# Last group norm moved ahead by two gate tiles, the mixed projection's pools split, its input tiles on another queue, x loads spread

## The chip, the cores and the metric

The kernel runs on one core of a Trainium2 chip. Times are device microseconds of that core. TensorE (PE in the profile) does the matrix products, VectorE (DVE) and ScalarE (ACT) the element-wise work, GpSimd (POOL) a few additions and part of the DMA issues, and SyncE (SP) issues DMAs only. A DMA is issued by one of these engines, in that engine's own instruction order: while the instruction at the head of a queue waits, those behind it wait as well.

## What is computed

One layer of a hybrid encoder for 384 tokens (256 of a prompt, 8 streams of 16 sampled tokens), model width 2048, all in float32:

```python
u = rmsnorm(x, g_mix_pre)
proj = u @ w_in                               # pool | z | xBC | dt | gates
a_pool = pool_mixer(pool part)                # windows 2, 4, 8, 16, then a map per group
a_ssd  = gated_rmsnorm(ssd_scan(...) , z)     # 8 groups of 512 channels, each normed by itself
merged = sigmoid(gA) * (a_pool @ w_pool_proj) + sigmoid(gB) * (a_ssd @ w_ssd_proj)
x = x + rmsnorm(merged @ w_out, g_mix_post)
x = x + rmsnorm(relu(rmsnorm(x) @ w_up)**2 @ w_down, g_mlp_post)
```

The scan also returns new states. The outputs are y and the new pool, convolution and scan states.

## The kernel before

**Products.** Each float32 operand is split into a high part h (rounded by ACT to a shorter float) and a rest l (subtracted by DVE); a product is the sum of three matmuls, h·h, h·l and l·h. A weight tile of 128 x 1024 is fetched by SP (`wfetch`, L61 to L64), its h is made by ACT (L70) and its l by DVE (L71). There are three buffers each for the fetched tile, h and l, so a fetch waits for the l of the tile three earlier. A "unit" is such a tile: `half` (L101 to L103) runs 24 matmuls on it, and a gate or projection tile of 128 channels has two units.

**Order of the work.** The framework plans one fixed order of instructions for each engine before the kernel runs, from the program order and its own estimates of time: an instruction that it believes ready can be put ahead of one that comes first in the program. An instruction that uses a tile of a new pool has its place in that order only behind the release of the older pools whose addresses it covers. At run time every instruction waits just for the tiles that it needs itself (pools with `reuse_waits="tile"`). `behind(ins)` adds an order edge and no wait: what is traced in its block stands behind `ins` on the same engine. `later()` does so behind the latest weight split that was noted in `cut`.

**Stages around the change.** (1) Eight scan groups g = 0 to 7, each with ten projection tiles. A group ends with `finish` (L917; a 512-channel norm: two matmuls for the sum over channels, L207 and L208, then ten dependent DVE instructions, L189 to L193 and L210) and `store` (L920: four DVE products, L925, into the z tiles, and four DMAs by POOL into `a_scr`, L928). For the last group this comes in the branch `g == G`: gate tiles 0 to 3 with the rest of the scan woven in, the last scan products, gate tiles 4 to 7, and then `finish(prev)` and `store(prev)`.

(2) The mixed projection, `a_ssd @ w_ssd_proj`. It is done by a seven-product scheme on 2 x 2 blocks: `quad` splits each step into seven "forms" (b11, b21, U, b22, W, V, X), and for each of eight pairs of channel tiles, gk = 0 to 7, and both column halves there is one quad: 112 forms of 6 or 12 matmuls (L1169 to L1171, N = 512). The forms are woven between the units of the gate tiles 8 to 12 and of twelve tiles of the other gate (`gate_b`, `gate_late`; `hook` runs 3 or 4 forms after each unit, the first three after the second tile's last unit). `load` in `quad` fetches four weight tiles by SP (L1130) and adds one more onto the first by an accumulating DMA of POOL (L1133), which makes U. `aload(gk)` reads one input tile `ax` from `a_scr` by four DMAs (L1229, on SP), `diffs` (L1235, DVE) forms its differences, and `refill` splits them (L1242 ACT, L1243 DVE). The places of these in `extra` are counted by t = 0 to 13 over the fourteen forms of one gk; W, V and X of a gk are refilled at t = 0 to 2 of that gk itself.

All tiles of stage 2 lie in one pool, `phe`, with the accumulators `acs` first (36,864 bytes in each partition), then `ax`, the split inputs, the gate tiles `gt` among them, and the weight tiles `wd` last. The pool lies over `phd`, the pool of the scan groups.

(3) The output projection, `moving` (L154 to L156), four column blocks nb with eight weight tiles `w_wo` each. Ahead of it POOL loads the three x tiles of 1 MB (L1428 and L1429). `gpo`, a scale vector, is fetched by SP at the start of each block (L1522) and scaled by ACT (L1523). The x tiles are first read by `residual` at the end of the fourth block.

Of the kernel before, what the change touches and what calls it, by code (L numbers as in the profile page):

```python
# [14 lines left out]
P = 128  # L15
# [18 lines left out]
def build(ctx, tc, io):  # L34
# [21 lines left out]
    def behind(ins):  # L56
        return nullcontext() if ins is None else tc.issue_after(ins.ins)

    cut = [None, None]

    def wfetch(src, name):  # L61
        w = wpool.tile([P, 1024], F32, tag="w", name=f"w_{name}")
        sy.dma_start(w, src)
        return w, name  # L64

    def wsplit(f):
# [10 lines left out]
    @contextmanager  # L77
    def later():
        with behind(cut[0]), behind(cut[1]):
            yield  # L80
# [502 lines left out]
    def gate_b(i, pool, tag, hook=None, bufs=None):  # L583
        ps = proj([io["w_gb"][i, q] for q in range(2)], xg, f"gb{i}", hook)
        t = pool.tile([P, T], F32, tag=tag, name=f"gbt{i}", **({"bufs": bufs} if bufs else {}))
        with later():
            v.tensor_tensor(halves(t), even_odd(ps), halves(rstd), ALU.mult)
            s.activation(t, t, AF.Sigmoid)
        gp.dma_start(gb_scr[i], t)

    with tc.tile_pool(name="phd", bufs=2, reuse_waits="tile") as pd, tc.tile_pool(
# [325 lines left out]
        def finish(D):  # L917
            D.bc = norm_bc(pd, D.ssum, 512, f"g{D.g}", last[0], D.parts)

        def store(D):  # L920
            bc = D.bc
            for j in range(4):
                i = D.g * 4 + j
                z = D.zs[j]
                v.scalar_tensor_tensor(  # L925
                    out=z, in0=z, scalar=vec[:, V_NRM + i : V_NRM + i + 1], in1=bc, op0=ALU.mult, op1=ALU.mult
                )
                gp.dma_start(a_scr[i], z)  # L928
# [15 lines left out]
        for g in range(G + 1):  # L944
            if g == G:
                S = prev.p[1]
                work = [
                    [lambda: xside(S)],
                    [lambda: hside(S), lambda: eside(S, 0)],
                    [],  # L950
                    [lambda: eside(S, 1)],
                    [lambda: dside(S)],
                    [lambda: expside(S)],
                    [lambda: fside(S, 0), lambda: fside(S, 1)],
                    [],
                ]
# [12 lines left out]
                state(prev.p[1])  # L969
                final(prev.p[1])  # L970
                for i in range(4, 8):
                    gate_b(i, pd, "cacc")
                prev.parts = None
                finish(prev)
                store(prev)
                break
            u0 = 17 + g * 10
            D = Pair()
# [138 lines left out]
    def split(w, name):  # L1117
        h = wpool.tile([P, 1024], F32R, tag="wh", name=f"wh_{name}")
        l = wpool.tile([P, 1024], F32R, tag="wl", name=f"wl_{name}")
        s.activation(h, w, AF.Copy)  # L1120
        v.tensor_tensor(l, w, h.bitcast(F32), ALU.subtract)
        return h, l

    def quad(nm, pool, acc, np_, fresh, unit, part, extra=lambda i: None):
# [92 lines left out]

    mpool = ExitStack()
    phe = ExitStack()
    pq = phe.enter_context(tc.tile_pool(name="phe", bufs=1, reuse_waits="tile"))  # L1220
    acc = pq.tile([P, 18, 512], F32, name="acs")
    KEYS = {"b11": (0,), "s2": (2,), "b21": (3, 5), "U": (6,), "b22": (8, 9), "W": (7,), "V": (1,), "X": (4,)}
    raw, slots = [], [{} for _ in range(8)]

    def aload(gk):
        x = pq.tile([P, 10, 2, P], F32, tag="ax", name=f"ax{gk}")
        for q in range(2):
            for p in range(2):
                sy.dma_start(x[:, q * 3 : q * 3 + 3, p], a_scr[gk * 4 + q * 2 + p].rearrange("p (s t) -> p s t", s=3))  # L1229
        raw.append(x)  # L1230

    def diffs(gk):
        x = raw[gk]
        for o, a, b in DIFFS:
            v.tensor_tensor(x[:, o], x[:, a], x[:, b], ALU.subtract)  # L1235

    def refill(gk, key):
        ss = KEYS[key]
        n = len(ss)
        src = raw[gk][:, ss[0] : ss[-1] + 1 : max(1, ss[-1] - ss[0])]  # L1240
        h, l = (pq.tile([P, n, 2, P], F32R, tag=f"a{a}{key}", name=f"a{a}{key}{gk}", bufs=2 if key == "s2" else 1) for a in "hl")
        s.activation(h, src, AF.Copy)  # L1242
        v.tensor_tensor(l, src, h.bitcast(F32), ALU.subtract)  # L1243
        for i, j in enumerate(ss):
            slots[gk][j] = (h[:, i], l[:, i])

    def sp_quad(gk, np_):
        def part(slot, k2):
            h, l = slots[gk][slot]
            return h[:, k2], l[:, k2]  # L1250

        def extra(i):
            t = np_ * 7 + i
            if gk and t < 3:
# [22 lines left out]
        return quad(f"sq{gk}_{np_}", pq, acc, np_, gk == 0, lambda i, nb: io["w_ssd"][nb, gk * 2 + i], part, extra)  # L1277

    todo, place = [], {}

    def fetch(n):
        if n not in place:
            place[n] = pq.tile([P, 1024], F32, tag="wd", name=f"mw{n}", bufs=7)
        gp.dma_start(place[n][:, :T], gb_scr[n])
        gp.dma_start(place[n][:, T : 2 * T], ma_scr[n])

# [67 lines left out]

    for i in range(8, 10):
        gate_b(i, pq, "gt", hook, 2)
    for i in range(4, KD):
        gate_late(i, hook)
    for i in range(10, 13):
# [65 lines left out]
        return y  # L1425

    blk = lambda i: slice(i * 512, i * 512 + 512)
    for b in range(3):  # L1428
        gp.dma_start(x1[:, b, :], io["x_tok"][b])  # L1429
    xs2 = []  # L1430

    def xtiles(pool, n):
# [6 lines left out]
    with tc.tile_pool(name="phf", bufs=1, side="right", reuse_waits="tile") as pf, tc.tile_pool(  # L1439
# [80 lines left out]
        for nb in range(4):  # L1520
            gpo = pf2.tile([P, 512], F32, tag="gpo", name=f"gpo{nb}", bufs=1)
            sy.dma_start(gpo, io["g_mix_post"][blk(nb)].partition_broadcast(P))  # L1522
            s.activation(gpo, gpo, AF.Copy, scale=-0.5)  # L1523
            o = [sstile(f"wo{nb}_{b}") for b in range(3)] if nb else o_first

            def scaled(b, nb, o, gpo):
                return v.tensor_tensor(hm[:, b, blk(nb)], o[b], gpo, ALU.mult)

            def done(b):
                q = pf2.tile([P, 512], F32, tag="q", name=f"q1_{nb}_{b}", bufs=1)  # L1530
                sq = lambda: s.activation(q, o[b], AF.Square, accum_out=st[:, b, nb : nb + 1])
                if nb < 3:
                    sq()
                    scaled(b, nb, o, gpo)
                    return
                act(sq)
                with behind(ca[0]), behind(cd[0]):
                    ys[b] = postnorm(pf2, st, b, "n1", doubled=True)
                ca[0], cd[0] = root[0], root[1]
                if b == 2:  # L1540
                    return
                for i in range(3):
                    residual(b, i)
                dve(lambda: scaled(b, nb, o, gpo))
                residual(b, 3)
                if b == 1:
                    square(0, 0)
# [386 lines left out]
```

## Time and profile before

| | |
|---|---|
| median of 3 runs | 2600.66 us (2598.7 to 2602.01) |
| the profiled execution | 2600.41 us, its span 2598.4 us |
| PE | 2575.4 us busy, 99% of the span |
| PEld (weight loads) | 2447.4 us, 94% |
| DVE | 1952.1 us, 75% |
| ACT | 1597.8 us, 61% |
| POOL | 424.0 us, 16% |
| DMA | 490.42 MB, 189 GB/s over the span |

PE is busy for nearly the whole span, so the table says little about where time could go. The windows view gives the busy time of each engine in chosen stretches together with the mean clock that was granted to TensorE (1.00 is full). The timeline lists instructions with their start, their length and, in brackets, the idle time of their engine before them and what ended it. Times in these views are in us from the start of the span.

### The profile page before, as it was taken

How to read it: one execution, taken by the hardware profiler on the slowest of the kernel's cores; microseconds unless marked ns; L12 is line 12 of the kernel's file. 1: busy time of each engine (PE TensorE's matmuls, PEld its weight loads, DVE VectorE, ACT ScalarE, POOL GpSimd, SP SyncE). 2: the span in 40 equal slices, each digit the busy share in tenths (PEclk: the TensorE clock that was granted, in tenths of full speed). 3: DMA queues.
4: the chain of work that ended last, by engine and by line, in shares of the span. 5: the costliest groups of instructions: out<-in, count | busy, mean ns of one | idle time of the engine just before them, and what ended most of it. 6: DMA issues, size and time to landing. Idle time of an engine off the chain costs nothing.

```text
span 2598.4 us, 41070 instructions
## 1 busy us (share of the span) xinstructions
PE 2575.4 (99%) x15589; PEld 2447.4 (94%) x15589; DVE 1952.1 (75%) x2763; ACT 1597.8 (61%) x2520; POOL 424.0 (16%) x622
## 2 busy tenths in 40 slices
PE   9999999999999999989999999999999999999998
PEld 9999999999999999978988988999999999999997
DVE  6676367999999999678888855767777777777766
ACT  6443355657565756467887634667667666666653
POOL 0000043445444544100000210000000000000000
PEclk9999999999999999999999999999999999999999
DMA  7444466666676676576766565655455554455434
GB/s 279 151 136 160 161 227 213 232 212 232 228 241 208 230 241 223 180 241 194 212 199 183 175 220 178 196 168 156 146 162 163 167 166 146 154 157 166 140 137 171
DMA packets 151189, 490.42 MB, mean 189 GB/s; under 512 B 21728, under 2 KB 36896, under 8 KB 145232
## 3 DMA queue, kind: packets, MB, share of 16 engines
q1 hardware_dynamic: 111312, 358.29, 40.9%
q0 software_dynamic: 32624, 114.70, 15.3%
q10 hardware_dynamic: 7056, 14.81, 1.8%
q8 instruction: 122, 2.00, 0.3%
q14 instruction: 75, 0.61, 0.1%
HBM read 437.85 MB, written 49.87 MB: 188 GB/s over the span
## 4 chain that ended last, share of the span: by engine, by line
PE 93%; DMA 2%; issue 2%; DVE 2%; ACT 1%; POOL 0%; SPq 0%; DVEq 0%; POOLq 0%; ACTq 0%
PE pj_up L101 6%; PE pj_up L102 6%; PE pj_up L103 6%; PE wd L1171 5%; PE wd L1170 5%; PE wd L1169 5%; PE pj_x L101 5%; PE pj_x L102 5%; PE pj_x L103 5%; PE pj_z L101 3%; PE pj_z L103 3%; PE pj_z L102 3%; PE sq L1170 2%; PE sq L1171 2%; PE sq L1169 2%
## 5 line engine op out<-in xcount | busy, mean ns | idle before, releaser
L101 PE MATMUL pj_up<-x1h,wh_up 128*128 128x384 f32 (+1 forms) x1024 | 333.7, 326 | 0.0
L102 PE MATMUL pj_up<-x1l,wh_up 128*128 128x384 f32 (+1 forms) x1024 | 333.5, 326 | 0.0
L103 PE MATMUL pj_up<-x1h,wl_up 128*128 128x384 f32 (+1 forms) x1024 | 333.5, 326 | 0.0
L70 ACT ACTIVATE wh_up<-w_up 128x1024 fp32r<-128x1024 f32 x126 | 133.1, 1057 | 219.2 <-PE pj_up L102 206.1
L101 PE MATMUL pj_x<-xgh,wh_x 128*128 128x384 f32 x768 | 252.0, 328 | 0.0
L103 PE MATMUL pj_x<-xgh,wl_x 128*128 128x384 f32 x768 | 250.4, 326 | 0.0
L102 PE MATMUL pj_x<-xgl,wh_x 128*128 128x384 f32 x768 | 250.4, 326 | 0.0
L71 DVE TENSOR_TENSOR wl_up<-w_up,wh_up 128x1024 fp32r<-128x1024 f32 x126 | 153.9, 1221 | 56.3 <-ACT wh_up L70 56.2
L102 PEld LDWEIGHTS pj_up<-x1l,wh_up 128*128 128x128 f32 x1024 | 193.6, 189 | 2.6
L101 PEld LDWEIGHTS pj_up<-x1h,wh_up 128*128 128x128 f32 x1024 | 193.6, 189 | 2.6
L103 PEld LDWEIGHTS pj_up<-x1h,wl_up 128*128 128x128 f32 x1024 | 193.6, 189 | 0.0
L101 PE MATMUL pj_z<-xgh,wh_z 128*128 128x384 f32 x512 | 167.0, 326 | 0.0
L103 PE MATMUL pj_z<-xgh,wl_z 128*128 128x384 f32 x512 | 166.9, 326 | 0.0
L102 PE MATMUL pj_z<-xgl,wh_z 128*128 128x384 f32 x512 | 166.9, 326 | 0.0
L1133 POOL DMA_DIRECT2D w_b_wd<-w_down x28 | 24.1, 862 | 773.4 <-DMA w_b_wd<-w_down 719.4
L101 PEld LDWEIGHTS pj_x<-xgh,wh_x 128*128 128x128 f32 x768 | 145.1, 189 | 2.1 <-issue 0.4
L103 PEld LDWEIGHTS pj_x<-xgh,wl_x 128*128 128x128 f32 x768 | 145.2, 189 | 0.0
L102 PEld LDWEIGHTS pj_x<-xgl,wh_x 128*128 128x128 f32 x768 | 145.2, 189 | 0.0
L71 DVE TENSOR_TENSOR wl_x<-w_x,wh_x 128x1024 fp32r<-128x1024 f32 x96 | 116.6, 1219 | 29.5 <-ACT wh_x L70 29.5
L70 ACT ACTIVATE wh_x<-w_x 128x1024 fp32r<-128x1024 f32 x96 | 100.3, 1051 | 60.8 <-PE pj_z L102 30.4
L1146 ACT COPY acc<-wd 128x512 f32<-128x512 f32 x200 | 116.6, 583 | 23.0 <-PE wd L1171 22.9
L1169 PE MATMUL wd<-wh_b_wd,fh 128*128 128x512 f32 x336 | 127.4, 379 | 0.0
(478 smaller groups left out, 7807.8 us busy)
## 6 DMA issues: line engine op xcount, KB each, us to landing
w_up<-w_up SPq DMA_DIRECT2D x128, 512.0 KB, 4.0
w_b_wd<-w_down SPq DMA_DIRECT2D x112, 512.0 KB, 4.4
w_x<-w_in SPq DMA_DIRECT2D x96, 512.0 KB, 3.8
w_z<-w_in SPq DMA_DIRECT2D x64, 512.0 KB, 4.1
w_b_sq<-w_ssd SPq DMA_DIRECT2D x64, 512.0 KB, 4.4
w_ga<-w_ga SPq DMA_DIRECT2D x32, 512.0 KB, 4.2
w_pp<-w_pp SPq DMA_DIRECT2D x32, 512.0 KB, 3.5
hs<-ssm POOLq DMA_DIRECT2D x16, 1024.0 KB, 7.7
```

Source lines behind the costliest of these rows:

```text
L70: cut[0] = s.activation(h, w, AF.Copy)
L71: cut[1] = v.tensor_tensor(l, w, h.bitcast(F32), ALU.subtract)
L101: te.matmul(out, wh, xh, start=first, stop=False, **how)
L102: te.matmul(out, wh, xl, start=False, stop=False, **how)
L103: return te.matmul(out, wl, xh, start=False, stop=last, **how)
L1133: gp.dma_start(w, unit(0, np_ * 2), accum_op=ALU.add)
L1146: s.copy(dst, o)
L1169: te.matmul(out, mh, vh, start=begin, stop=False, skip_group_check=held)
L1170: te.matmul(out, mh, vl, start=False, stop=False, skip_group_check=held)
L1171: te.matmul(out, ml, vh, start=False, stop=end, skip_group_check=held)
```

## The change

1. `finish(prev)` of the last group comes behind gate tile 5 (the sixth) and `store(prev)` behind gate tile 6, no longer behind gate tile 7.
2. The pool `phe` becomes four, in the order of their addresses: `phe` (ax, gt, pt), `php` (split inputs), `phq` (weight tiles), `phr` (the accumulators).
3. `aload` for gk > 0 is issued by POOL, no longer by SP, and stands at t = 4, no longer t = 5. The first one stays on SP, and every weight fetch on SP that is traced after gate tiles 8 and 9 (`ahead`) stands behind its last DMA.
4. `split`, the weight split of the forms, notes its two instructions in `cut`, and `diffs` and `refill` run inside `later()`.
5. The x tiles are loaded by SP, behind the latest weight fetch, inside the second and third column blocks.

```diff
-    cut = [None, None]
+    cut, ahead, fetched = [None, None], [None], [None]
 
     def wfetch(src, name):
         w = wpool.tile([P, 1024], F32, tag="w", name=f"w_{name}")
-        sy.dma_start(w, src)
+        with behind(ahead[0]):
+            fetched[0] = sy.dma_start(w, src)
         return w, name
...
                 final(prev.p[1])
+                prev.parts = None
                 for i in range(4, 8):
                     gate_b(i, pd, "cacc")
-                prev.parts = None
-                finish(prev)
-                store(prev)
+                    if i == 5:
+                        finish(prev)
+                    if i == 6:
+                        store(prev)
                 break
...
     def split(w, name):
-        s.activation(h, w, AF.Copy)
-        v.tensor_tensor(l, w, h.bitcast(F32), ALU.subtract)
+        cut[0] = s.activation(h, w, AF.Copy)
+        cut[1] = v.tensor_tensor(l, w, h.bitcast(F32), ALU.subtract)
...
-    pq = phe.enter_context(tc.tile_pool(name="phe", bufs=1, reuse_waits="tile"))
-    acc = pq.tile([P, 18, 512], F32, name="acs")
+    pq, pqf, pqw, pqa = (phe.enter_context(tc.tile_pool(name=f"ph{a}", bufs=1, reuse_waits="tile")) for a in "epqr")
+    acc = pqa.tile([P, 18, 512], F32, name="acs")
...
     def aload(gk):
         x = pq.tile([P, 10, 2, P], F32, tag="ax", name=f"ax{gk}")
         for q in range(2):
             for p in range(2):
-                sy.dma_start(x[:, q * 3 : q * 3 + 3, p], a_scr[gk * 4 + q * 2 + p].rearrange("p (s t) -> p s t", s=3))
+                i = (gp if gk else sy).dma_start(
+                    x[:, q * 3 : q * 3 + 3, p], a_scr[gk * 4 + q * 2 + p].rearrange("p (s t) -> p s t", s=3)
+                )
         raw.append(x)
+        return i
...
             if gk and t < 3:
-                refill(gk, ("W", "V", "X")[t])
+                with later():
+                    refill(gk, ("W", "V", "X")[t])
...
-            if t == 5:
+            if t == 4:
                 aload(gk + 1)
-            elif t == 9:
-                diffs(gk + 1)
-            elif t == 10:
-                refill(gk + 1, "b11")
-                refill(gk + 1, "s2")
-            elif t > 10:
-                refill(gk + 1, ("b21", "U", "b22")[t - 11])
+            with later():
+                if t == 9:
+                    diffs(gk + 1)
+                elif t == 10:
+                    refill(gk + 1, "b11")
+                    refill(gk + 1, "s2")
+                elif t > 10:
+                    refill(gk + 1, ("b21", "U", "b22")[t - 11])
...
-    aload(0)
+    ax0 = aload(0)
...
     for i in range(8, 10):
         gate_b(i, pq, "gt", hook, 2)
+    ahead[0] = ax0
     for i in range(4, KD):
         gate_late(i, hook)
...
-    for b in range(3):
-        gp.dma_start(x1[:, b, :], io["x_tok"][b])
...
+            def xload(b):
+                with behind(fetched[0]):
+                    sy.dma_start(x1[:, b, :], io["x_tok"][b])
+
+            late_x = {1: {1: lambda: xload(0), 5: lambda: xload(1)}, 2: {3: lambda: xload(2)}}.get(nb)
...
                 5 if nb == 3 else 0,
-                None,
+                late_x,
```

The split inputs are taken from `pqf` and the weight tiles (also `mw`) from `pqw`.

More of the change, by code (lines that the diff above doesn't have):

```diff
@@ L1240, in refill @@
         src = raw[gk][:, ss[0] : ss[-1] + 1 : max(1, ss[-1] - ss[0])]
-        h, l = (pq.tile([P, n, 2, P], F32R, tag=f"a{a}{key}", name=f"a{a}{key}{gk}", bufs=2 if key == "s2" else 1) for a in "hl")
+        h, l = (pqf.tile([P, n, 2, P], F32R, tag=f"a{a}{key}", name=f"a{a}{key}{gk}", bufs=2 if key == "s2" else 1) for a in "hl")
         s.activation(h, src, AF.Copy)
@@ L1266, in extra @@
                 return
-            if t == 5:
+            if t == 4:
                 aload(gk + 1)
-            elif t == 9:
-                diffs(gk + 1)
-            elif t == 10:
-                refill(gk + 1, "b11")
-                refill(gk + 1, "s2")
-            elif t > 10:
-                refill(gk + 1, ("b21", "U", "b22")[t - 11])
-        return quad(f"sq{gk}_{np_}", pq, acc, np_, gk == 0, lambda i, nb: io["w_ssd"][nb, gk * 2 + i], part, extra)
+            with later():
[6 more added lines that the diff above has]
+                    refill(gk + 1, ("b21", "U", "b22")[t - 11])
+        return quad(f"sq{gk}_{np_}", pqw, acc, np_, gk == 0, lambda i, nb: io["w_ssd"][nb, gk * 2 + i], part, extra)
     todo, place = [], {}
@@ L1282, in fetch @@
         if n not in place:
-            place[n] = pq.tile([P, 1024], F32, tag="wd", name=f"mw{n}", bufs=7)
+            place[n] = pqw.tile([P, 1024], F32, tag="wd", name=f"mw{n}", bufs=7)
         gp.dma_start(place[n][:, :T], gb_scr[n])
```

## The prediction

> **What bounds the kernel now.** First the page, for the share of PE.
>
> ```profile
> span 2598.4 us, 41070 instructions
> ...
> PE 2575.4 (99%) x15589; PEld 2447.4 (94%) x15589; DVE 1952.1 (75%) x2763; ACT 1597.8 (61%) x2520; POOL 424.0 (16%) x622
> ```
>
> PE is idle for 23 us of 2598.4. An edit that adds and removes no product, as this one, can return only such idle time, and time in which PE ran below its clock. So next the windows view, cut so that PE's gaps stand alone; its columns are the length, the busy time of PE, PEld, DVE, ACT and POOL with the number of instructions, the granted clock, the DMA share and GB/s.
>
> ```profile
> 0.00:20.00 20.00, 16.90 (x86) 13.79 (x87) 10.92 (x19) 11.31 (x18) 0.41 (x5) 1.00 0.91 342
> 20.00:1100.00 1080.00, 1079.94 (x7642) 1063.18 (x7641) 852.23 (x1338) 601.05 (x1066) 343.05 (x495) 1.00 0.61 206
> 1100.00:1125.00 25.00, 17.32 (x76) 14.79 (x75) 15.83 (x26) 11.84 (x21) 5.52 (x9) 0.80 0.97 313
> 1125.00:1210.00 85.00, 85.00 (x442) 78.08 (x441) 69.07 (x83) 64.11 (x99) 7.99 (x12) 1.00 0.71 206
> 1210.00:1215.00 5.00, 4.17 (x17) 2.85 (x16) 3.88 (x5) 5.00 (x10) 0.00 (x0) 1.00 0.27 84
> ...
> 1300.00:1310.00 10.00, 9.68 (x48) 8.04 (x47) 10.00 (x15) 8.88 (x14) 1.57 (x3) 1.00 0.43 127
> ...
> 1390.00:1400.00 10.00, 8.64 (x39) 6.63 (x37) 10.00 (x14) 8.19 (x13) 1.25 (x2) 1.00 0.45 145
> ...
> 1530.00:1545.00 15.00, 13.86 (x62) 11.28 (x61) 7.68 (x8) 6.88 (x12) 0.00 (x0) 1.00 0.54 157
> 1545.00:2580.00 1035.00, 1035.00 (x5597) 969.25 (x5597) 721.63 (x937) 666.92 (x944) 27.86 (x35) 1.00 0.51 160
> 2580.00:2599.00 19.00, 9.92 (x46) 8.34 (x45) 13.55 (x30) 3.02 (x9) 0.00 (x0) 0.90 0.45 166
> ```
>
> Idle PE: 3.10 us in the first 20 us and 9.08 in the last 19, which the change does not touch; 0.06 up to 1100; then 7.68 (place A, the start of the mixed projection), 0.83, 0.32 and 1.36 (B, inside it, together 2.51) and 1.14 (C, the output projection). From 1545 to 2580 there is none. The windows left out have PE busy throughout. At A the clock is 0.80 too, so the PE timeline is read there.
>
> ```profile
> 1105.93 0.33 PE L103 MATMUL pj_gb<-xgh,wl_gb 128*128 128x384 f32 x1
> 1113.09 0.80 PE L1169 MATMUL sq<-wh_b_sq,ahb 128*128 128x512 f32 x1 [6.83 <-ACT wh_b_sq L1120]
> ...
> 1115.16 0.80 PE L1170 MATMUL sq<-wl_b_sq,ahb 128*128 128x512 f32 x1 [0.85 <-DVE wl_b_sq L1121]
> ...
> 1120.45 0.42 PE L1171 MATMUL sq<-wh_b_sq,alb 128*128 128x512 f32 x1
> 1120.70 0.38 PE L1169 MATMUL sq<-wh_b_sq,ahb 128*128 128x512 f32 x1
> ...
> 1123.72 0.38 PE L1171 MATMUL sq<-wh_U_sq,alU 128*128 128x512 f32 x1
> ```
>
> ```profile
> 1113.00:1120.40 7.40, 6.46 (x14) 0.50 1.05 239
> ```
>
> The last gate matmul starts at 1105.93; gate matmuls follow one another every 0.163 us, so the first product of the mixed projection could start at 1106.09. It starts at 1113.09, after 6.83 us of idle, waits 0.85 us more at 1115.16, and the fourteen matmuls up to 1120.45 run at half clock. From 1120.70 to 1123.72 fourteen intervals take 3.02 us, or 0.2157 each. Without a stall the fifteenth would start at 1106.09 + 14 x 0.2157 = 1109.11; it starts at 1120.45. **A costs 11.34 us**: 7.00 to the first start, 0.85, and 3.49 of slow clock.
>
> Who is late at A? ACT's high parts of the first weights, by PE's wait. ACT stood behind the input splits, these behind DVE, and DVE here:
>
> ```profile
> 1074.78 0.56 DVE L587 TENSOR_TENSOR gbt<-pj_gb,rstd 128x384 f32<-128x384 f32 x1 [1.75 <-PE pj_gb L103]
> ...
> 1090.38 0.56 DVE L587 TENSOR_TENSOR gbt<-pj_gb,rstd 128x384 f32<-128x384 f32 x1 [1.70 <-PE pj_gb L103]
> ...
> 1099.23 2.21 DVE L925 SCALAR_TENSOR_TENSOR zs<-zs,vec,ny_g 128x384 f32<-128x384 f32 x4
> ...
> 1109.20 0.56 DVE L587 TENSOR_TENSOR gbt<-pj_gb,rstd 128x384 f32<-128x384 f32 x1 [4.41 <-DMA a_scr<-zs]
> ```
>
> ```profile
> 1101.73 7.34 DMA a_scr<-zs
> ```
>
> ```profile
> 1112.00 1.99 ACT L1120 ACTIVATE wh_b_sq<-w_b_sq 128x1024 fp32r<-128x1024 f32 x2
> ```
>
> Gate tile 9's buffer lies on the z tile 3 of group 7 (add up the tiles of `phe` in the order of first use), so its product at 1109.20 waited for the `a_scr` store that reads that tile, issued as the last of four at 1101.73 and 7.34 us on the way. Everything of `diffs` and `refill` for gk = 0 stands behind it on DVE, and the weight splits on ACT from 1112.00 stand behind these.
>
> **The change, part by part.**
>
> *The norm and the store (A).* From gate tile 7's product (1090.38) to the end of the four z products (1099.23 + 2.21 = 1101.44) it is 11.06 us. After the change the chain starts two gate tiles earlier, at 1074.78, that is 15.60 us: z products done by about 1085.8. The ten norm instructions are the same; they move into a stretch where DVE had gaps of 1.7 us before each gate product, and delay a weight split by less than they did before. The four `a_scr` issues move with them, ahead of gate tile 7's store on POOL:
>
> ```profile
> 1092.03 0.54 POOL L589 DMA_DIRECT2D gb_scr<-gbt  x1 [7.26 <-ACT gbt L588]
> 1100.14 2.13 POOL L928 DMA_DIRECT2D a_scr<-zs  x4 [7.58 <-DVE zs L925]
> ```
>
> So they are issued at about 1084.5 to 1086.7, and with 7.34 us the last lands by 1094. What waits for it now? By the new order of pools, ax lies over the scan's xT, xD, BT and cbc tiles and gt over cbc, all read for the last time by the scan's last products, which run ahead of gate tile 4. The weight tiles start 37,376 bytes into the area, and the first weight that is used, b11, takes the seventh buffer (as in the old kernel's order of buffers), over the z tiles 0 to 3 of group 7. So SP's fetch of b11 inherits the wait, and b21, b22 and the next gate weights queue behind it: issue 1094, landing 4.4 later, split 2.2 later (ACT 1.0, DVE 1.2), that is 1100.6 at the latest, against 1106.09. 5.5 us are spare.
>
> ```profile
> w_b_sq<-w_ssd SPq DMA_DIRECT2D x64, 512.0 KB, 4.4
> ...
> w_wo<-w_out SPq DMA_DIRECT2D x32, 512.0 KB, 3.6
> ...
> w_b_sq<-w_ssd POOLq DMA_DIRECT2D x16, 512.0 KB, 8.7
> ...
> ax<-a_scr SPq DMA_DIRECT2D x32, 192.0 KB, 4.2
> ...
> x<-x_tok POOLq DMA_DIRECT2D x3, 1024.0 KB, 9.9
> ...
> ppt<-pp_scr POOLq DMA_DIRECT2D x12, 192.0 KB, 5.2
> ...
> gpo<-g_mix_post SPq DMA_DIRECT2D x4, 256.0 KB, 4.6
> ```
>
> *ax of gk = 0 (A).* Its tiles' places in the queues come behind `phd`'s release, whose last user is now gate tile 7's store on POOL at 1092.03, no longer the a_scr stores at 1102.3. If SP really had to wait for that, ax would land at 1097 (4.2) and the chain of differences and splits, 1109.20 to 1113.99 = 4.8 us before, would end at 1102. `ahead` keeps the gate weights, which overtook ax in the old order, behind it. They are needed 30 matmuls after 1106.09 = 1112.6, and can be fetched from 1097 on. Not on the path.
>
> *U (A).* The third form needs POOL's accumulation: the first weight lands at about 1093, the accumulation is issued behind gate tile 8's store (its product one tile, 7.80 us, after 1090.38, and 1.1 us for product and sigmoid: 1099.3), lands 8.7 us plus 0.5 for the store's issue later, 1108.5, split by 1110.7. U's first matmul is due at 1106.09 + 24 x 0.2157 = 1111.27. Just in time, and 8.7 is a median: I charge 0.5, bounds 0 (issued as soon as the weight is there) and 2. So A returns 10.8 of 11.34.
>
> *ax of the other seven gk, refills behind the splits (B).* In the old order refills stand early, since the plan believed that ax would be there:
>
> ```profile
> ACT ahs L1242 <- DMA ax<-a_scr: 8.7, 5, 3.1
> ```
>
> ```profile
> 1299.39 0.42 ACT L1242 ACTIVATE ahs<-ax 128x256 fp32r<-128x256 f32 x1 [3.06 <-DMA ax<-a_scr]
> ```
>
> ACT stands 8.7 us at the head of `ahs` (refill of s2), with the weight splits behind it; the gap at 1300 follows the longest of these waits, 3.06 us up to 1299.39, and the two others stand behind one as well. Now the refill is put behind the split of its form, at t = 10, so ACT cannot be held. Need comes four forms later; a form takes about 3.1 us (66 matmuls x 0.2157 over 7 forms, plus a unit of 3.9 us for every 3.6 forms). `diffs` add 1.75 us at t = 9, against two forms (6.2 us) by which the three l buffers let the splits run ahead. Also SP loses 28 issues that waited for the previous ax and held weight fetches. On POOL, an issue costs 2.13 / 4 = 0.53 us: 15 us over a stage of some 350 us (112 forms) in which POOL is busy 9% (7.99 of 85 us from 1125 on). I take 2.0 of 2.51; bounds 2.51, and -1.5 for a new order with short waits of its own.
>
> By the Trainium skill (SBUF — State Buffer, § SBUF: two separate sides) a DMA from POOL's queue is the wrong one here: its descriptors are written by GpSimd, which some DVE operations lock out, and a 620 ns transfer took 3100 ns there. The trace has `ppt`, issued by POOL, landing in 5.2 us with DVE busy 81% (69.07 of 85), against 4.2 for SP's `ax`, so no such factor shows; by the rule four loads would come some 10 us later, the limit of rival 4 would fall from 17.1 to 7 us, and its 2619 would be the likelier time. The row decides, and rival 4 keeps the chance that it has without the rule.
>
> *x loads (C).*
>
> ```profile
> 1514.66 1.58 POOL L1429 DMA_DIRECT2D x<-x_tok  x3 [10.84 <-DVE ml L1304]
> ```
>
> ```profile
> 1528.94 0.63 ACT L1523 ACTIVATE gpo<-gpo 128x512 f32<-128x512 f32 x1 [8.06 <-DMA gpo<-g_mix_post]
> ...
> 1538.17 0.63 ACT L1523 ACTIVATE gpo<-gpo 128x512 f32<-128x512 f32 x1 [4.70 <-DMA gpo<-g_mix_post]
> ```
>
> Three loads of 1 MB on POOL go beside the first `gpo`; ACT waits 8.06 us for it and 4.70 for the second, with weight splits behind, and PE loses 1.14. Without them `gpo` should take about its median 4.6. The second wait partly stays. On SP the x loads stand between `w_wo` fetches (3.6 us landing). A weight is fetched three tiles ahead, 3 x 3.88 us (18 matmuls each) less the split, 9 us; one x load in front costs 3.3 us (three took 9.9 together) to 9.9. The first is hidden, the second would cost 4.5 us for each of three. I take 0.5 returned, bounds 1.14 and -5, nearer to the first because the other transfers of this stage are few (DMA share 0.54).
>
> *Four pools, the later place of x's fetch, the note in `cut` for gate products.* No instruction is added. A gate product stands now behind the split of the last form traced; its bank is due two gate tiles later. Nothing.
>
> **Sum.** 10.8 + 2.0 + 0.5 = 13.3 us from the profiled execution's 2600.41 (2598.4 of span and 2.0 around it): 2587.1. The median of the runs is 0.25 higher; I say **2587.4 us**, 0.5% faster. If all of A, B and C went: 2585.4.
>
> **Rivals.**
> 1. *The wait moves to b11's fetch.* If the plan leaves the z products behind gate tile 7's product, they end near 1093.2, the stores are issued behind 1092.03 and land by 1101.4, b11 lands at 1105.8 and is split at 1108: 2 us of idle, and between nothing and 3.49 of slow clock, since 0.83 idle kept 1.00 and 6.83 gave 0.50. Time 2589 to 2592.5, say 2590.5. For it: the address of b11. Against: ten short DVE instructions that are ready by 1084.
>    The Trainium skill (TensorE: Matmul & The Clock Gate, § Part 1: The HAM clock gate) has the clock halve after an idle window of about 3.4 us; by it the slow part is zero here and the time 2589. Both gaps of this trace agree.
> 2. *U decides the start.* In the old POOL queue the accumulation stands behind gate tile 9's store. Kept so: that product at 1106.7, sigmoid and store 1107.8, accumulation landing 1117.4, split 1119.7, due 1111.27: 8.4 idle, slow clock, A as before. Time 2600.4 - 2.5 = 2598, no change. Against: that gate product is now traced behind U's own split.
> 3. *Only A goes.* The forced places of refills, or x loads, cost what they save: 2600.4 - 10.8 = 2589.6, to 2593.
> 4. *Slower: ax late on POOL's queue, DVE stands at `diffs`.* POOL waits long for gate products:
>
> ```profile
> POOL ma_scr L1327 <- DVE gat L1326: 163.6, 11, 21.6
> ```
>
>    From t = 2 to t = 9 there are 21.7 us, with the splits' lead 27.9; four issues and a landing of 8.7 leave 17.1 for a hold-up. At the longest, 21.6, PE loses 4.5 in each of seven groups: 2587.4 + 31.5 = 2619. It turns slower than now where the hold-up passes 19 us each time. Against: the mean of the 11 waits is 14.9, and the four issues can be placed ahead of the waiting store, as a fresh ax buffer comes free at t = 2.
>
> **Chances.** Forecast 0.68, rivals 0.11, 0.07, 0.10, 0.04. A measurement of this kernel tells about 0.2% (5.2 us) from no change. Forecast and rivals 1 and 3 are faster by more: 0.89, of which I move 0.02 to the same for mishaps that add up. Same 0.08, slower 0.05. Range: down to 2584 (everything, less a run's scatter of 1.5), up to 2597, which takes in rivals 1 and 3 with C's bound of -5, and leaves out 2 and 4.
>
> **What would show it.** Right: PE's gap at the first `sq` matmul under 1 us with clock 1.00; the last `a_scr` store landing before 1095; no wait of `ahs` for ax; ACT's first wait for `gpo` about 3 us. Wrong: idle at A with clock 0.5; SP waiting for a DMA of `a_scr` at b11 past 1101; DVE waiting for ax at L1235; gaps of several us among the `wo` matmuls behind an x load.

## The result, and the profile after

The changed kernel takes 2588.36 us (median of 5 runs, 2587.65 to 2588.84) against 2599.41 us (2598.20 to 2602.01) for the kernel before in the same comparison: a ratio of 0.9956, 95% interval 0.9942 to 0.9971. The profiled execution took 2588.24 us.

The page of after, then its windows view:

```profile
span 2586.5 us, 41046 instructions
...
PE 2572.9 (99%) x15589; PEld 2448.1 (95%) x15589; DVE 1951.8 (75%) x2763; ACT 1599.2 (62%) x2520; POOL 446.4 (17%) x647
```

```profile
1100.00:1125.00 25.00, 25.00 (x134) 23.23 (x133) 17.07 (x20) 15.39 (x21) 5.90 (x8) 1.00 0.99 324
1180.00:1185.00 5.00, 4.41 (x25) 3.88 (x24) 5.00 (x8) 5.00 (x10) 1.11 (x2) 1.00 0.49 170
...
1270.00:1275.00 5.00, 4.04 (x19) 3.00 (x18) 5.00 (x6) 5.00 (x10) 0.00 (x0) 1.00 0.35 111
1315.00:1320.00 5.00, 3.99 (x19) 2.92 (x18) 5.00 (x7) 5.00 (x9) 0.00 (x0) 1.00 0.44 161
1360.00:1365.00 5.00, 4.51 (x22) 3.31 (x20) 5.00 (x8) 4.92 (x9) 0.00 (x0) 1.00 0.45 130
1405.00:1415.00 10.00, 9.55 (x48) 8.14 (x47) 10.00 (x14) 9.56 (x16) 1.46 (x2) 1.00 0.63 188
1530.00:1545.00 15.00, 15.00 (x72) 13.12 (x71) 4.90 (x4) 3.69 (x5) 0.00 (x0) 1.00 0.57 210
```

A is gone: PE is busy for all of 1100 to 1125 at a clock of 1.00, and its gap at C is gone too. But inside the mixed projection there are new gaps, about one per gk, 45 us apart (0.59, 0.96, 1.01, 0.49 and 0.45 here, with a small one at 1225), where before had three places with 2.51 us together. In each of these windows DVE is busy throughout, and ACT nearly so.

How much each place is worth is better read from starts than from idle time. The groups of three matmul lines, before and then after; the last column but one holds the first and the last start:

```profile
L1169 PE MATMUL sq<-wh_b_sq,ahb x160: 378/379/796, 1113.1 to 1461.8; 128*128 128x512 f32 x160
...
L154 PE MATMUL wo<-wh_wo,mh x162: 379/379/483, 1494.2 to 1602.5; 128*128 128x512 f32 x162
...
L101 PE MATMUL pj_up<-x1h,wh_up x1024: 275/326/409, 1624.6 to 2527.1; 128*128 128x384 f32 x169, 128*128 128x256 f32 x2
```

```profile
L1172 PE MATMUL sq<-wh_b_sq,ahb x160: 379/379/379, 1106.1 to 1451.8; 128*128 128x512 f32 x160
...
L155 PE MATMUL wo<-wh_wo,mh x162: 379/379/463, 1484.2 to 1590.5; 128*128 128x512 f32 x162
...
L102 PE MATMUL pj_up<-x1h,wh_up x1024: 275/326/409, 1612.7 to 2515.2; 128*128 128x384 f32 x169, 128*128 128x256 f32 x2
```

| stretch | before | after | difference |
|---|---|---|---|
| to the first product of the mixed projection | 1113.1 | 1106.1 | -7.0 |
| from there to the first `wo` matmul | 381.1 | 378.1 | -3.0 |
| from there to the first `pj_up` matmul | 130.4 | 128.5 | -1.9 |
| from there to the end of the span | 973.8 | 973.8 | 0 |

The second stretch of before holds 0.85 us of idle and 3.49 us of slow clock that belong to A. So A returned 7.0 + 4.34 = 11.34 us, B became 4.34 - 3.0 = 1.3 us longer, and C returned 1.9: 11.9 us, the difference of the spans (2598.4 - 2586.5).

Why is C's 1.9 more than its 1.14 of idle? The timeline of PE in after, at one of the new gaps:

```profile
1318.47 0.38 PE L1172 MATMUL sq<-wh_V_sq,ahs 128*128 128x512 f32 x1
1319.86 0.43 PE L104 MATMUL pj_ga<-xgh,wl_ga 128*128 128x384 f32 x1 [1.01 <-DVE wl_ga L72]
1320.12 0.33 PE L102 MATMUL pj_ga<-xgh,wh_ga 128*128 128x384 f32 x1
```

After the matmul at 1318.47 the next could start 0.216 us later, at 1318.69. It starts 1.17 us late, and only 1.01 of it is recorded as idle, since a matmul's record is 0.38 long; the one behind it starts 0.26 later instead of 0.163. The stall costs 1.27 us, 0.26 more than its idle time. Counted in the same way, the three stalls of C in before (up to 1531.83, 1539.80 and 1541.06) cost 0.49, 0.31 and 1.15 us, together 1.95: that is C's 1.9.

What ends this gap is the l of the gate weight, `wl_ga`; so it is with the gaps at 1182 and 1274, and the three hold 2.44 us of idle. The two last, smaller, end with a gate weight's h and with V's l. The timeline of DVE ahead of `wl_ga` (after; the number in brackets is idle time, and where there is none DVE had no pause):

```profile
1307.75 1.23 DVE L1124 TENSOR_TENSOR wl_U_sq<-w_b_sq,wh_U_sq 128x1024 fp32r<-128x1024 f32 x1 [1.25 <-ACT wh_U_sq L1123]
1308.89 0.42 DVE L1241 TENSOR_TENSOR ax<-ax 128x256 f32<-128x256 f32 x1
...
1310.96 1.42 DVE L1241 TENSOR_TENSOR ax<-ax 128x256 f32<-128x256 f32 x4
...
1314.57 0.42 DVE L1249 TENSOR_TENSOR alb<-ax,ahb 128x256 fp32r<-128x256 f32 x1
1314.91 0.42 DVE L1249 TENSOR_TENSOR als<-ax,ahs 128x256 fp32r<-128x256 f32 x1
1315.24 1.22 DVE L1124 TENSOR_TENSOR wl_W_sq<-w_b_sq,wh_W_sq 128x1024 fp32r<-128x1024 f32 x1
...
1317.52 0.69 DVE L1249 TENSOR_TENSOR alb<-ax,ahb 128x512 fp32r<-128x512 f32 x1
...
1318.59 1.22 DVE L72 TENSOR_TENSOR wl_ga<-w_ga,wh_ga 128x1024 fp32r<-128x1024 f32 x1
```

From 1307.75 to the end of `wl_ga` at 1319.81 DVE works without a pause: 12.1 us, of which differences and refills take 0.42 + 1.42 + 0.42 + 0.42 + 0.69 = 3.4. PE waited for it until 1319.86.

At A, the timelines of POOL, SP and DVE in after:

```profile
1084.90 0.54 POOL L929 DMA_DIRECT2D a_scr<-zs  x1 [7.92 <-DVE zs L926]
...
1086.22 1.61 POOL L929 DMA_DIRECT2D a_scr<-zs  x3
...
1096.93 0.91 POOL L1136 DMA_DIRECT2D w_b_sq<-w_ssd  x1 [3.23 <-DMA w_b_sq<-w_ssd]
1101.49 0.56 POOL L590 DMA_DIRECT2D gb_scr<-gbt  x1 [3.65 <-ACT gbt L589]
```

```profile
1087.99 2.68 SPq L1232 DMA_DIRECT2D ax<-a_scr  x4
1090.71 2.84 SPq L1133 DMA_DIRECT2D w_b_sq<-w_ssd  x4
1093.65 1.29 SPq L64 DMA_DIRECT2D w_ga<-w_ga  x2
```

```profile
1084.00 2.20 DVE L926 SCALAR_TENSOR_TENSOR zs<-zs,vec,ny_g 128x384 f32<-128x384 f32 x4
...
1107.29 1.23 DVE L1124 TENSOR_TENSOR wl_U_sq<-w_b_sq,wh_U_sq 128x1024 fp32r<-128x1024 f32 x1 [2.67 <-ACT wh_U_sq L1123]
```

The stores are issued from 1084.90 on, the first ax and weight loads stand ahead of the gate weights on SP, and U's accumulation goes out before gate tile 8's store. The first four of SP's form weight fetches, one of which waited 0.6 us for the stores, are out by 1093.55. The z products are done at 1086.2, and U's l at 1108.52.

### The profile page after: what moved, and what is told of

Same layout as the page of the kernel before. It is cut to its first block, busy times and chain, and to the rows that moved or that the text cites. A ratio compares the mean times of both kernels' runs of the same rounds, so it can differ in the third digit from the quotient of the medians.

```text
span 2586.5 us, 41046 instructions
## 1 busy us (share of the span) xinstructions
PE 2572.9 (99%) x15589; PEld 2448.1 (95%) x15589; DVE 1951.8 (75%) x2763; ACT 1599.2 (62%) x2520; POOL 446.4 (17%) x647
## 4 chain that ended last, share of the span: by engine, by line
PE 96%; DVE 2%; ACT 1%; issue 1%; DMA 1%; DVEq 0%; POOL 0%; ACTq 0%; POOLq 0%
PE pj_up L102 6%; PE pj_up L104 6%; PE pj_up L103 6%; PE wd L1173 5%; PE wd L1174 5%; PE wd L1172 5%; PE pj_x L102 5%; PE pj_x L103 5%; PE pj_x L104 5%; PE pj_z L104 3%; PE pj_z L102 3%; PE pj_z L103 3%; PE sq L1173 2%; PE sq L1174 2%; PE sq L1172 2%; PE pj_pp L102 2%
```

## Experiments

Beside each median stands the ratio to the kernel before, run beside it on the same chip, with its 95% interval.

### The changed kernel again

> The changed kernel unaltered, beside the kernels that are compared with it. All theories: 2588.4 us, six gaps at the gate weights' l inside the mixed projection, 3.6 us of idle together.

2588.92 us (0.9952, 0.9939 to 0.9964): the figure with which the altered versions below are compared.

### The norm's place alone

```diff
 # the kernel before
...
-                finish(prev)
-                store(prev)
+                    if i == 5:
+                        finish(prev)
+                    if i == 6:
+                        store(prev)
```

> The kernel before with the first part of the change alone (finish behind gate tile 5, store behind gate tile 6; old pool, old queues). Theory (the place of the norm sets A): the a_scr stores land by 1095, so gate tile 9's product, which still lies over a z tile, no longer waits for them; PE's gap at the first product of the mixed projection is under 1 us with the clock at 1.00, B (2.5 us) and C (1.1 us) stay as before: 2600.4 - 10.8 = 2589.6 us. Rival (the pools must be reordered as well, since in the old order ax and the weights still stand behind the release of the scan's pool): a gap of 3 us or more is left at A, 2593 to 2598 us.

2597.19 us (0.9983, 0.9974 to 0.9992), between 2593.7 and 2601.9. The time is the rival's. The first product now starts on time (1106.73, right behind the last gate matmul), but three gaps follow, 0.35, 0.78 and 1.72 us. Is the rival's reason right, too? The timeline of SP shows what is late:

```profile
1089.66 4.23 SPq L63 DMA_DIRECT2D w_ga<-w_ga  x2
1093.99 2.59 SPq L1231 DMA_DIRECT2D ax<-a_scr  x4
1096.62 2.65 SPq L1132 DMA_DIRECT2D w_b_sq<-w_ssd  x5
```

Two gate weights, which are needed last, go first; SP waits 4 us in them for buffers, and ax and the form weights stand behind, 6 us later than in after. POOL's accumulation for U then goes out at 1104.34, no longer at 1096.93. U's l ends the second gap, and the third ends with a gate weight's l, whose h stands on ACT behind a wait of 3.85 us for U's weight. That can be an order on SP of its own (theory S below) or a consequence of the pools, the rival's reason (theory P).

### Without the order edge on SP, and with one pool

```diff
 # the changed kernel
-    ahead[0] = ax0
```

> The changed kernel without the order edge that holds SP's gate weight fetches behind the first ax load. With the norm moved alone 2.85 us of idle were left at A; there SP issued two gate weights at 1089.7, the second of which waited 4 us for its buffer, and only then ax (1094.0) and the form weights (1096.6). Theory S (that order on SP is what is left): without the edge the gap of about 2.9 us and some slow clock in part of the executions come back, 2591 to 2595 us. Theory P (the four pools put ax and the weights ahead by themselves): no gap, 2588.5 us.

2594.85 us (0.9975, 0.9965 to 0.9985): 5.9 us slower than the changed kernel, as theory S has it. SP issues `w_ga` at 1089.79 for 4.23 us, and `ax` only at 1094.32; PE's timeline and windows at U:

```profile
1114.29 0.48 PE L1172 MATMUL sq<-wh_U_sq,ahU 128*128 128x512 f32 x1 [1.98 <-ACT wh_U_sq L1123]
...
1115.55 0.48 PE L1173 MATMUL sq<-wl_U_sq,ahU 128*128 128x512 f32 x1 [0.78 <-DVE wl_U_sq L1124]
```

```profile
1112.00:1116.00 4.00, 1.24 (x5) 0.61 (x4) 1.73 (x3) 1.53 (x3) 0.00 (x0) 1.00 1.03 374
1116.00:1122.00 6.00, 4.98 (x15) 3.69 (x14) 5.97 (x6) 4.82 (x7) 0.58 (x1) 0.50 0.71 187
```

The first products start on time (1106.9); U, the third form, comes late, and slow clock follows. With one pool in place of four:

```diff
 # the changed kernel
-    pq, pqf, pqw, pqa = (phe.enter_context(tc.tile_pool(name=f"ph{a}", bufs=1, reuse_waits="tile")) for a in "epqr")
+    pq = phe.enter_context(tc.tile_pool(name="phe", bufs=1, reuse_waits="tile"))
+    pqf = pqw = pqa = pq
```

> The changed kernel with the one old pool (accumulators first, weight tiles last) in place of the four; the order edge on SP stays. Theory S: ax and the form weights are still issued ahead of the gate weights, no gap above 1 us at A, 2588.5 us. Theory P: ax and the weights have their places in the order only behind the release of the scan's pool and come late, a gap of 2 us or more at A, 2591 to 2598 us.

2588.42 us (0.9949, 0.9935 to 0.9962), no gap at A; SP issues `ax` at 1086.35 and the form weights at 1089.04. Theory S holds and P falls: the four pools are worth nothing that can be measured.

### The norm's place and the edge on SP, nothing else

```diff
 # the kernel before, with the norm's place as above
...
+        with behind(ahead[0]):
             sy.dma_start(w, src)
...
+    ahead[0] = ax0
```

> The kernel before with the earlier norm and the order edge on SP (gate weights behind the first ax load), and nothing else of the change: one pool, ax by SP, free refills, x loads on POOL ahead of the output projection. Theory S (these two are all that A needs): no gap above 1 us at A with the clock at 1.00; ACT's waits for ax inside the mixed projection (8 to 11 us) and its first wait for gpo (8 us or more) stay; 2600.5 - 11.3 = 2589 us, within 2588 to 2591. Rival (refills behind the splits are needed at A as well, since gk = 1's first refill can stand ahead of U's split, as in the kernel with free refills, where 2.6 us of idle came back at A): a gap of 2 to 4 us and 2592 to 2596 us.

2589.99 us (0.9959, 0.9945 to 0.9973). The windows show A busy throughout, as in after, and the old gaps at B:

```profile
1100.00:1125.00 25.00, 25.00 (x134) 23.23 (x133) 19.39 (x26) 15.68 (x22) 2.88 (x4) 1.00 0.97 320
1200.00:1205.00 5.00, 4.22 (x19) 3.20 (x19) 4.70 (x6) 5.00 (x8) 0.00 (x0) 1.00 0.33 111
1375.00:1390.00 15.00, 13.34 (x66) 11.05 (x65) 12.96 (x18) 10.93 (x16) 1.45 (x2) 1.00 0.53 165
```

ACT's waits for ax (8.1 us) and its longest wait for `gpo` (8.0) stay as expected. Theory S holds. So two of the edits carry 10 us, nearly all that the whole change brings; what the other parts add together is about 1 us, and the two intervals overlap.

### The norm late again, all else as changed

```diff
 # the changed kernel
-                    if i == 5:
-                        finish(prev)
-                    if i == 6:
-                        store(prev)
+                finish(prev)
+                store(prev)
```

> The changed kernel with finish and store put back behind gate tile 7. Theory: the wait for a_scr moves to SP's fetch of b11, whose buffer lies over the z tiles. The stores are issued at about 1101.5 to 1104 and land at 1107 to 1111; b11 lands 4.4 later and is split 2.2 later, 1114 to 1118, against 1106.1: a gap of 8 to 12 us, slow clock for 3.5 more, and the first wait of SP at the form weights is for a DMA of a_scr, several us. 2588.4 + 11.5 to 15.5 = 2600 to 2604 us, no faster than the kernel before. Rival (the order of the pools alone removes A, since gate tile 9 no longer lies over a z tile): a gap under 2 us and 2588 to 2591 us.

2597.66 us (0.9987, 0.9978 to 0.9996). The mechanism is the theory's, its price 2 to 6 us less. The waits of SP and the timeline of PE:

```profile
SPq L1131 <- DMA a_scr<-zs: 15.5, 2, 14.9
```

```profile
1112.56 0.80 PE L1170 MATMUL sq<-wh_b_sq,ahb 128*128 128x512 f32 x1 [6.63 <-ACT wh_b_sq L1121]
```

SP stands 14.9 us at a form weight's fetch for `a_scr`, with all other fetches behind it, and PE starts 6.63 us late, with a clock of 0.50 up to 1117. The wait on the z tiles had moved from gate tile 9's product to this fetch, and without the earlier norm it decides there as before.

### The store's place alone

```diff
 # the changed kernel
-                    if i == 6:
+                    if i == 7:
                         store(prev)
```

> The changed kernel with store (z products and a_scr issues) behind gate tile 7, finish still behind gate tile 5: a part of the way back to the norm behind gate tile 7, which left a gap of 6.6 us. Theory (A now hangs on the landing of a_scr, which SP's fetch of b11 inherits): issues at 1092.6 to 1094.7, landing at 1098 to 1102, b11 split at 1104.5 to 1108.6 against 1105.6: a gap between 0 and 3 us, SP's wait for a_scr 5 us or longer, clock 1.00, 2588.4 to 2591.5 us. Rival (the plan puts the z products where they are ready, wherever they are traced): a_scr issues before 1089, no gap, 2588.4 us.

2588.21 us (0.9951, 0.9937 to 0.9964): the rival holds. POOL issues the first store at 1085.05, ahead of gate tile 6's own store, as in after. The plan puts the z products where it believes them ready; of the two places that the edit changes, `finish` decides. This kernel says nothing on how late the stores may land.

### Refills not held behind the splits

```diff
 # the changed kernel
-                with later():
-                    refill(gk, ("W", "V", "X")[t])
+                refill(gk, ("W", "V", "X")[t])
...
-            with later():
-                if t == 9: ...
+            if t == 9: ...
```

> The changed kernel with differences and refills outside of later(), so that they are not held behind the weight splits; the queue of ax and its place at t = 4 stay. Theory (the order edges make the new gaps, and the earlier ax by POOL's queue is what ended the old waits for ax): the gaps at the gate weights' l fall to a sum under 1 us, ACT does not wait for ax, 2585.5 us. Rival (the order edges are what ended the old waits): ACT waits for ax again, some 8 us in all, gaps of 2 to 3 us that lie elsewhere than now, 2587.5 us or more.

2596.34 us (0.9980, 0.9971 to 0.9988): the rival, and worse than it said. ACT's waits:

```profile
ACT ahs L1248 <- DMA ax<-a_scr: 18.1, 6, 6.1
```

Again refills stand ahead of splits, and ACT waits for ax although POOL issues it early. One of these waits (6.1 us, up to 1108.57, ahead of U's split) brought 2.6 us of idle back at A. So the order edges do what ended the waits of before, and they are needed. They have a part in the new gaps: behind A, those at `wl_ga` hold 0.63 us here and 2.44 in after, but gaps behind the l of form weights come in their place.

### ax on SP's queue

```diff
 # the changed kernel
-                i = (gp if gk else sy).dma_start(
+                i = sy.dma_start(
```

> The changed kernel with all ax loads on SP's queue (t = 4 and the order edges stay). Theory (the order edges, not the queue, ended ACT's waits for ax): no wait of ahs for ax; SP's weight fetches stand behind ax loads that wait for the last split of X, which costs 0 to 1.5 us: 2588.4 to 2590 us. Rival (POOL's queue is needed, so that ax is issued early): DVE waits for ax at the differences, 5 us or more in all, and PE's idle time inside the mixed projection rises above 6 us: 2591 us or more.

2588.54 us (0.9952, 0.9939 to 0.9964). ACT and DVE have no wait for ax, and the gaps at `wl_ga` are the same: the theory holds, and the queue makes no difference.

### x loads on POOL ahead of the output projection

```diff
 # the changed kernel
+    for b in range(3):
+        gp.dma_start(x1[:, b, :], io["x_tok"][b])
...
-                late_x,
+                None,
```

> The changed kernel with the three x loads on POOL ahead of the output projection, as in the kernel before. Theory (these loads hold the first gpo, and with it ACT): ACT's first wait for gpo is about 8 us again, PE has gaps among the wo matmuls, from the first wo matmul to the first matmul of the MLP it is 130.4 us as before, not 128.5: 2588.4 + 1.9 = 2590.3 us. Rival (the gaps at C came from the order of the work behind the mixed projection, which other parts changed): 128.5 us, 2588.4 us.

2590.07 us (0.9959, 0.9946 to 0.9973), 1.2 us above the changed kernel run beside it, where the theory has 1.9; its shortest run (2589.77) is longer than the longest of that one (2589.47). The profiled execution was the longest of its five (2593.99), and shows what can come on top. ACT's waits, PE's timeline and windows:

```profile
ACT gpo L1532 <- DMA gpo<-g_mix_post: 17.8, 4, 10.5
```

```profile
1523.97 0.48 PE L155 MATMUL wo<-wh_wo,mh 128*128 128x512 f32 x1 [1.58 <-ACT wh_wo L71]
...
1525.22 0.48 PE L156 MATMUL wo<-wl_wo,mh 128*128 128x512 f32 x1 [0.78 <-DVE wl_wo L72]
```

```profile
1522.00:1526.00 4.00, 1.64 (x7) 0.88 (x6) 2.05 (x3) 3.60 (x9) 0.00 (x0) 1.00 0.02 7
1526.00:1529.00 3.00, 3.00 (x9) 2.40 (x8) 2.13 (x3) 0.88 (x1) 0.00 (x0) 0.53 0.70 225
```

### The differences spread over three forms, and sooner

```diff
 # the changed kernel
...
             with later():
-                if t == 9:
-                    diffs(gk + 1)
+                if 6 < t < 10:                       # two, two, one
+                    diffs(gk + 1, DIFFS[t * 2 - 14 : t * 2 - 12])
```

> The changed kernel with the five differences of each gk spread over t = 7, 8 and 9 (two, two, one), no longer all at t = 9. Theory (the 3.6 us of new gaps inside the mixed projection come from a stretch of DVE in which five differences, three splits, three sums and three refills follow one another without a pause, so that the next gate weight's l is late): the differences move into DVE's pauses some 6 us earlier, the stretch is 1.7 us shorter, the six gaps of 0.4 to 1.0 us fall to a sum of 1.0 us or less, 2588.4 - 2.6 = 2585.8 us. Rival (the gaps come from the order edges, by which refills must stand ahead of that gate weight's split, wherever the differences are): the six gaps stay at 3 us or more, 2588 us.

2583.91 us (0.9931, 0.9919 to 0.9944). The theory's cause holds and its price was too low: the idle time left behind `wl_ga` is 0.8 us in two gaps, the stretch from the first product to the first `wo` matmul 373.4 us (378.1 in after), and the time 5.0 us below the changed kernel.

```diff
 # the version above; the slice of DIFFS moves with t
-                if 6 < t < 10:
+                if 5 < t < 9:
...
-                elif t == 10:
-                    refill(gk + 1, "b11")
+                elif t == 9:
+                    refill(gk + 1, "b11")
+                elif t == 10:
                     refill(gk + 1, "s2")
```

> The changed kernel with the differences at t = 6, 7 and 8 (two, two, one) and the refill of b11 at t = 9, s2 still at t = 10; with t = 7 to 9 and both refills at t = 10 it was 2583.9 us, with 0.76 us of gaps left behind the gate weights' l. Theory (what is left is the same stretch of DVE work, still too long by 0.4 us): the last gaps go, 2583.1 to 2583.5 us. Rival (the lead is used up: ax has not landed at t = 6, and DVE waits for it ahead of weight splits): new gaps, 2584.5 us or more.

2582.15 us (0.9926, 0.9913 to 0.9940), the fastest of all: 18 us below the kernel before, 6.8 below the changed one. Its windows, and the group of first products and of `wo`:

```profile
1125.00:1270.00 145.00, 145.00 (x750) 133.38 (x749) 123.44 (x150) 117.51 (x182) 21.00 (x30) 1.00 0.67 196
1270.00:1275.00 5.00, 4.90 (x29) 4.52 (x28) 4.39 (x6) 5.00 (x9) 2.04 (x3) 1.00 0.81 245
1275.00:1425.00 150.00, 150.00 (x772) 137.42 (x771) 128.06 (x152) 121.33 (x192) 24.79 (x38) 1.00 0.70 204
```

```profile
L1172 PE MATMUL sq<-wh_b_sq,ahb x160: 378/380/380, 1105.7 to 1445.7; 128*128 128x512 f32 x160
...
L155 PE MATMUL wo<-wh_wo,mh x162: 378/380/463, 1478.1 to 1584.4; 128*128 128x512 f32 x162
```

From the first product to `wo` it is 372.4 us: 5.7 less than in after, whose gaps showed 3.6 us of idle, and 4.4 less than in before without its stall at A (381.1 - 4.34), where B showed 2.51. DVE does not wait for ax, so the rival falls; the theory's gaps go, and the gain is about 1 us more than it said.

## Why the prediction was right, and where not

The sum was 13.3 us; the spans differ by 11.9. That the time came out 1 us from the forecast (2588.4 against 2587.4) is luck. B fell 3.3 us short of its term, A and C gave 0.5 and 1.4 more than theirs, and the kernel before ran at 2599.41 in this comparison, 1.25 below the median that the forecast starts from. The time lies 1.0 us from the forecast and 1.2 from rival 3's 2589.6, where only A goes; the stretches tell them apart, not the time.

**A, 10.8 forecast, 11.34 returned.** The chain of the norm went as worked out: z products done at 1086.2 (said 1085.8), stores from 1084.90 (1084.5). b11's fetch inherited the wait, as said, for 0.6 us. U was the step feared, and 0.5 charged: the accumulation was put behind gate tile 8's store, but the plan issued it ahead (1096.93 instead of 1099.3), and U's l was done at 1108.52, 2.7 us before its due time, so nothing was to pay. What the prediction missed is that two edits are needed. It worked A out from the norm's place, and of ax and the order edge on SP it said "Not on the path"; without the edge the kernel takes 2594.85 us, and with the norm's place alone 2597.19. The step that fell short looked at when the gate weights are needed, and not at what stands behind them: SP waits 4 us for their buffers, with ax and the form weights behind. That the pools cost nothing was right (2588.42 with one).

**B, +2.0 forecast, -1.3 measured.** The sign was wrong; the lower bound of -1.5, for a new order with short waits of its own, held it. That refills behind the splits end ACT's waits for ax was right, and free refills showed 18.1 us of these waits. The step that failed is the comparison of the 1.75 us of differences with the lead of the form weights' l, two forms. The instruction that came late was another one on the same engine, the gate weight's l, and what counts for it is the whole unbroken stretch ahead of it, 12.1 us of DVE work. Taking the differences out of this stretch returned 5.0 us, and 6.8 when they and one refill came sooner still. And the place was under-sized: against the fastest version B had lost 4.4 us in before, not 2.51.

**C, 0.5 forecast, 1.9 returned.** That is beyond the upper bound of 1.14, which was C's idle time; by starts C had cost 1.95. The mechanism was right; with the loads on POOL the long waits for `gpo` were back (17.8 us of ACT in the profiled execution) and the median was 1.2 us higher. ACT's waits for it in after:

```profile
ACT gpo L1530 <- DMA gpo<-g_mix_post: 9.7, 4, 3.6
```

The longest, the second, is 3.6 us (8.06 before), and the first 2.3 (about 3 forecast). The charge for the x loads on SP, up to 4.5 us each, was too high: they landed in 6.6 us (9.9 on POOL, three together), and no `wo` matmul waited.

**The rivals.** The first (the wait moves to b11's fetch) is what the kernel with the late norm does. The second (U decides) has its outcome in the kernel without the edge, but not its reason: there POOL issues U's accumulation at 1103.78, ahead of gate tile 8's store at 1106.31, and it is late since the form weight itself was. The third, that only A goes, is close to the truth: B and C together gave 0.6. The fourth, ax late on POOL, did not come: the loads landed in 3.1 us (median; 3.5 when SP issued them), DVE waited for none of them, and SP's queue did as well (2588.54). By the Trainium skill (SBUF — State Buffer, § SBUF: two separate sides) a DMA from POOL's queue waits for its descriptors while DVE runs certain operations, those in a 2-port mode. No run here shows such a wait, though DVE was busy 85% of the time (128.06 of 150 us) in the fastest kernel, whose loads from POOL landed in 3.0 us, the median; nor does any show which of DVE's operations here would be of that kind.

## What to carry to other kernels

Count a stage's loss by the starts of its instructions, from one landmark to the next, before an edit is priced: idle time showed little more than half of what was to be had at B. When work is forced to a later place, look for the longest stretch without a pause on its engine and for what stands at the end of it; spreading five short instructions over three places was worth nearly half as much as the whole change. In a queue of loads, one early request that must wait for its buffer holds everything behind it (4 us here), so an edge that orders two kinds of loads can decide what an earlier producer is worth: the earlier norm returned 4.3 us alone and 10.0 with the edge.

## What was not expected of the hardware

**The clock can fall after short, broken idle.** Two gaps of 1.58 and 0.78 us, 1.25 us apart from start to start, were followed by 0.53 from 1526 to 1529 (x loads on POOL); 1.98 and 0.78 us by 0.50 from 1116 to 1122 (no edge on SP); 0.42 and 1.79 us by 0.50 from 1206 to 1209 (refills not held); 6.63 us in one by 0.50 likewise. Gaps of 0.78 and 1.72 us, 3.4 apart, left it at 1.00 in the profiled execution with the norm's place alone, whose other executions were up to 8.2 us longer at a mean clock down to 0.997, where the profiled one had 0.999. The Trainium skill (TensorE: Matmul & The Clock Gate, § Part 1: The HAM clock gate) has the clock halve after an idle window of about 3.4 us that runs freely. Of these, only the 6.63 us were that long. Summed over the 3.4 us that hold most of it, the idle time was 2.36, 2.76 and 2.21 us in the three broken cases where the clock fell, and 1.73 where it stayed. A window that must be mostly idle, and not wholly, would fit these four rows; no run here shows the window itself.

**A stall costs more than its idle time**, 0.26 us each at the gap at 1319.86: 0.16 because the record of a matmul is longer than the interval between two, 0.10 because the first interval after the stall is longer. The Trainium skill (Perfetto Trace Analysis, § Identifying the Most-Contended Engine) calls the busy share of matmuls no good measure of how close a kernel is to the roofline, since they are pipelined. The runs agree: PE stood at 99% both with and without 12 us of stalls and slow clock.

**An issue on POOL has no fixed price.** Four ax loads took 2.99 us there, 0.75 each, where the four `a_scr` stores took 0.54 each; the estimate of 0.53 for ax was too low, and it cost nothing.
